# Expert stage of a two-block network: another transpose for short experts, and a third matrix half in high and low parts

## The chip, the cores and the metric

One Trainium2 chip, one of its cores. The metric is device time in microseconds of one execution of the whole program. Three runs of the kernel before took 1997.23, 2000.67 and 2002.16 us; their median is 2000.67 us.

## The reference, cut to what matters

256 tokens of width 1024 pass through two blocks. The change lies in the last large stage of the second block, a mixture of 8 experts, each of which has three matrices of 1024 x 3584, 1024 x 3584 and 3584 x 1024 in float32 (44 MB an expert, 352 MB in all):

```python
def moe_swiglu(h, w_router, w1, w3, w2):
    t = h.reshape(B * S, D)                                  # 256 x 1024
    logits = (t @ w_router).astype(jnp.float32)              # 8 experts
    top_vals, top_idx = lax.top_k(logits, TOP_K)             # TOP_K = 2
    top_w = jax.nn.softmax(top_vals, axis=-1)
    gates = jnp.sum(jax.nn.one_hot(top_idx, N_EXPERTS_2) * top_w[..., None], axis=1)
    out = jnp.zeros_like(t)
    for e in range(N_EXPERTS_2):
        out = out + gates[:, e:e + 1] * ((jax.nn.silu(t @ w1[e]) * (t @ w3[e])) @ w2[e])
    return out.reshape(B, S, D)
```

So 512 (token, expert) pairs are spread over 8 experts, some of which get more than 64 tokens and some fewer.

## The kernel before, in words

**Numbers in two parts.** TensorE takes float32 in a fast single pass only as fp32r, a float32 with a shortened mantissa. To keep precision the kernel splits an operand into `hi` (ScalarE copies it to fp32r, L99) and `lo` (VectorE subtracts `hi` from it, L100); `K.split` (L88) does both. A product is then hi·hi + hi·lo + lo·hi. A plain float32 product needs no split, but each of its matmuls goes through the array several times.

**Half-experts.** The stage, `moe` (L1508), handles each expert e in two halves s of 1792 hidden columns: 16 half-experts, n = 2e + s. For each there are three kinds of work, cut into jobs of two weight tiles of 128 x 1792 (896 KB each):
- *up*, 8 jobs: four for w1, then four for w3 (`up`, L1615, by `piece`, L1601). Each weight tile is loaded by a DMA on SP's queue (L85) into one of `RAW` = 9 places, split into one of 4 `whi` and one of 4 `wlo` places, and multiplied with the gathered token columns `xg`, which were split before. The four banks of results are copied out by ScalarE (`evict`, L1825): `gs` after w1, `us` after w3.
- *turn*, 4 groups of up to 4 column blocks (`turn`, L1634): `gs` and `us` are transposed on TensorE into two PSUM banks; then `turned` (L1816) makes silu of the one on ScalarE (L1822), multiplies it by the other on VectorE (L1823), and writes the block of `hd`, of which there is one place.
- *down*, 4 jobs (`down`, L1620): the weight tiles of w2 stay float32, are not split, and are multiplied with `hd` by plain float32 matmuls (L1629). Their place among the 9 is held until those matmuls are done.

**Short and long form.** The counts of the tokens are known only at run time. `arms` (L1594) makes a branch on TensorE alone: `many` (over 64 tokens) or `few`. For few tokens, the gathered columns lie so that token s of the first 64 is column 2s; `piece` then picks the 64 hi and the 64 lo columns as one stationary operand of 128, and two matmuls, with w hi and w lo, do what takes three in the long form. The result has 128 rows, 64 from hi and 64 from lo, whose sum is wanted. In `few`, `turn` (L1639) therefore doesn't transpose by the identity: it multiplies by `both` (L1520), in which column 2s has ones at rows s and 64 + s, and the other columns are zero, as a plain float32 matmul. So each transposed block comes out already summed. In `many` it is a plain transpose (L1641). `down` in `few` uses 64 stationary columns, and lets matmuls alternate between the two halves of the PSUM rows; the two halves are added when the result is sent back to the tokens (`transposed`, L1643, and `finish`, L1669).

**Order.** The list `jobs` (L1783) has, for each half-expert n: the 4 jobs of w1, the 4 of w3, and then the 4 down jobs of half-expert n - 1. `ahead` loads and splits one job ahead of the job being multiplied. The turn groups of n - 1 are put in front of the 4 w1 jobs of n; for even n they are branches of their own, so the scheduler may set the first group in the middle of the down jobs of n - 2. A scheduler sets the final order on each engine; ScalarE, VectorE and SP then work strictly in that order, waiting on semaphores. PSUM has 8 banks: 4 for an up product, 2 for a turn group and, for half of the time, 2 for the running down sums of an expert.

Of the kernel before, what the change touches and what calls it, by code (L numbers as in the profile page):

```python
# [8 lines left out]
F32 = mybir.dt.float32  # L9
# [10 lines left out]
P = 128  # L20
# [1105 lines left out]
ORD = (0, 1, 2, 3)  # L1126
RAW = 9


class Block2:  # L1130
# [378 lines left out]
    def moe(self, cap=P):  # L1509
# [8 lines left out]
        iota = iota_row(K, self.pool, P)  # L1518

        both = self.T([P, P])  # L1520
        nc.gpsimd.memset(both[:, 1::2], 0.0)
        nc.vector.tensor_tensor(both[:, 0::2], K.ident[:, :HALF], K.ident[:, HALF:], op=ADD)
        up_of = lambda n, e, s, k: a[n][0, e, k * P:(k + 1) * P, s * MS:(s + 1) * MS]
# [96 lines left out]
        def down(few, s, hd, acc, j, w):  # L1620


            c0 = c = j % 4 * MS
            while c < c0 + MS:
                c1 = min((c // 512 + 1) * 512, c0 + MS)
                r, h = divmod(c // 512, 2)
                o = slice((r + h) % 2 * HALF, (r + h) % 2 * HALF + HALF) if few else slice(0, P)
                n = 2 if few else 1
                mm(acc[h][o, c % 512:c % 512 + c1 - c], hd[:, j // 4 * R + r, ::n], w[0][:, c - c0:c1 - c0],  # L1629
                   start=s == 0 and j < 4 and r < n and c % 512 == 0,  # L1630
                   stop=s == NS - 1 and j > 3 and r >= R - n and c1 % 512 == 0)
                c = c1

        def turn(few, rows, pt, c0):  # L1634

            for c in range(c0, min(c0 + 4, 2 * R)):
                z = rows[:, c // R * (MS // 2) + c % R:(c // R + 1) * (MS // 2):R]
                if few:
                    mm(pt[:, (c - c0) * P:(c - c0 + 1) * P], z, both, start=True, stop=True)  # L1639
                else:  # L1640
                    nc.tensor.transpose(pt[:, (c - c0) * P:(c - c0 + 1) * P], z, K.ident)  # L1641

# [131 lines left out]
        def take(n, e, s, k, **how):  # L1774
            w = K.load(down_of(e, s, k) if n == "down" else up_of(n, e, s, k), 1, MS)
            if n == "down":
                return k, [w[:, 0]]
            b = lambda z: z.rearrange("p k (b q) -> p (k b) q", b=4)
# [4 lines left out]
        for i in range(E * NS + 1):  # L1783
# [3 lines left out]
            if i:  # L1787
                jobs += [("down", *divmod(i - 1, NS), (q, q + 1)) for q in range(0, 8, 2)]
        taken = {}
# [14 lines left out]
        for t in range(NT):  # L1804
            with K.behind(K.last):
                top2_weights(K, self.tmp, *tops[t][:2], iota, comb[:, t, :])
                nc.gpsimd.tensor_scalar(x[:, t, :], x[:, t, :], ALPHA, None, op0=MUL)
        most, mosti = self.T([P, 1]), self.T([P, 1], I32)
        nc.vector.tensor_reduce(most, cnt, axis=AX.X, op=MAX)
# [6 lines left out]
        def turned(i, c, pts):  # L1816

            n = min(4, 2 * R - c) * P
            if c == 0:
                hT[i] = self.W([P, 2 * R, P], "hd", F32, 1)  # L1820
            sg = self.W([P, 512], "sg", bufs=1)
            nc.scalar.activation(sg[:, :n], pts[0][:, :n], AF.Silu)  # L1822
            nc.vector.tensor_tensor(hT[i].rearrange("p c s -> p (c s)")[:, c * P:c * P + n], sg[:, :n], pts[1][:, :n], op=MUL)  # L1823

# [6 lines left out]
        for n, (name, e, s, ks) in enumerate(jobs):  # L1831
# [4 lines left out]
            if name == "down":  # L1836
                if s == 0 and q == 0:
                    accs[e] = [K.ps() for _ in range(2)]
                if i == E * NS - 1 and q == 0:
                    for c in range(0, 2 * R, 4):  # L1840
# [3 lines left out]
                arms(e, lambda few: [down(few, s, hT[i], accs[e], *t) for t in tiles])  # L1844
                if s == NS - 1 and q == 4:
                    hotT = transposed(e, gs[e][1])
                if s == NS - 1 and q == 6:
                    if e == E - 1:
# [109 lines left out]
```

## Time and profile before

| | |
|---|---|
| median of 3 runs | 2000.67 us |
| the profiled execution | 1999.19 us, of which the span of the profile is 1997.6 us |
| TensorE matmul (PE) busy in the span | 1843.4 us, 92% |
| VectorE (DVE) busy | 1133.8 us, 57% |
| ScalarE (ACT) busy | 929.9 us, 47% |
| DMA | 546.58 MB, mean 274 GB/s |
| TensorE's mean granted clock | 0.958 of full |

The expert stage runs from about 930 us to 1957 us of the span. Of its 8 experts, 0, 1 and 4 ran the long form and 2, 3, 5, 6, 7 the short one (lines L1613 and L1641 against L1610 and L1639). In this document, **stretch n** is the time from the eviction of `us` of half-expert n - 1 to that of half-expert n. It holds mostly the down jobs of n - 2, the turns of n - 1 and the up jobs of n:

| stretch | down | turn | up | us |
|---|---|---|---|---|
| 1 to 4 | many | many | many, many, many, few | 246.6 in all |
| 5 | many | few | few | 68.9 |
| 6 | few | few | few | 59.5 |
| 7 | few | few | few | 57.3 |
| 8 | few | few | many | 66.7 |
| 9 | few | many | many | 60.7 |
| 10 | many | many | few | 61.7 |
| 11 | many | few | few | 68.8 |
| 12 to 15 | few | few | few | 233.7 in all |
| the end | few (two) | few | none | 43.7 |

In odd stretches, VectorE and ScalarE also send the finished expert back to its tokens, and the next expert's tokens are gathered.

How to read the rows below. A row of a table of *windows* has: start:end of the window and its length in us; then for each engine its busy us in it and, in brackets, how many instructions ran (PE is matmuls, PEld weight loads); then the granted clock of TensorE (1.00 is full), the mean busy share of the DMA engines and what they moved in GB/s. A row of a *timeline* has: start and duration in us, engine, line, operation, output <- inputs, shapes, how many in a row, and in square brackets the idle time before it and what ended that. A row of the *chain of waits* has start, us, and what the end of the program hung on in that time. A row of *groups by line and shape* has the line, engine, operation, output <- inputs, shapes and the count; after the bar, busy us and the mean ns of one, and after the second bar the idle time before them and what ended it. A row of *waits* has who waited for whom, us in total, times, and the longest.

### The profile page before, as it was taken

To read this page: it belongs to the slowest core of one execution; us is meant where nothing else is said; L and a number is where in the kernel's file an instruction comes from. 1 tells how busy PE (TensorE), PEld (TensorE's weight loads), DVE (VectorE), ACT (ScalarE), POOL (GpSimd) and SP (SyncE) were. 2 spreads that over 40 slices of the span, in tenths; PEclk is the share of its full clock that TensorE was granted. 3 is DMA by queue.
4 is the path that set the end of the run, shared out by engine and by line. 5 is a ranking of instruction groups with operands and counts; after the bars stand their busy time and mean duration, and the time that the engine had idled before them with its cause. 6 is when DMAs were issued, how large, how long until landed. Compare 5 with 4: busy or idle time off the path is not lost. (4 is left out here: it accounts for less than half of the span.)

```text
span 1997.6 us, 27678 instructions
## 1 busy us (share of the span) xinstructions
PE 1843.4 (92%) x11023; PEld 1450.1 (73%) x11023; DVE 1133.8 (57%) x1395; ACT 929.9 (47%) x1222; POOL 169.8 (9%) x251
## 2 busy tenths in 40 slices
PE   7988698877999999987999999999999999999997
PEld 6878464323779998776877677877878678787875
DVE  4765542111986555887756436656557455675635
ACT  6444341101474443555746445545555445565533
POOL 2051210000400000324100000000000000000002
PEclk9989789889999999998999999999999999999999
DMA  7000579999655554415888989899989898999982
GB/s 221 29 1 1 193 292 407 421 421 397 243 179 175 190 190 148 169 43 219 323 299 318 327 273 376 319 362 395 360 326 400 306 361 308 387 376 359 405 318 106
DMA packets 131002, 546.58 MB, mean 274 GB/s; under 512 B 13568, under 2 KB 46475, under 8 KB 118540
## 3 DMA queue, kind: packets, MB, share of 16 engines
q1 hardware_dynamic: 126604, 539.21, 71.6%
q10 hardware_dynamic: 3952, 3.84, 0.6%
q8 instruction: 129, 2.11, 0.4%
q0 software_dynamic: 272, 1.05, 0.2%
q14 instruction: 45, 0.37, 0.1%
HBM read 543.01 MB, written 1.05 MB: 272 GB/s over the span
## 5 line engine op out<-in xcount | busy, mean ns | idle before, releaser
L100 DVE TENSOR_TENSOR wlo<-raw,whi 128x1792 fp32r<-128x1792 f32 (+2 forms) x412 | 681.0, 1694 | 291.5 <-ACT whi L99 290.2
L99 ACT ACTIVATE whi<-raw 128x1792 fp32r<-128x1792 f32 (+3 forms) x436 | 582.1, 1382 | 175.6 <-DMA raw<-in_exp_w_dram 59.2
L1610 PE MATMUL ps<-wlo,xg 128*128 128x256 f32 (+1 forms) x960 | 266.5, 308 | 17.0 <-DVE wlo L100 16.7
L1629 PE MATMUL ps<-raw,hd 128*64 128x512 f32 (+3 forms) x1024 | 275.4, 541 | 0.9 <-DVE hd L1823 0.9
L1610 PE MATMUL ps<-whi,xg 128*128 128x256 f32 (+1 forms) x960 | 266.7, 308 | 0.0
L1613 PE MATMUL ps<-whi,xg 128*128 128x512 f32 (+1 forms) x768 | 225.3, 373 | 0.0
L1629 PEld LDWEIGHTS ps<-raw,hd 128*64 128x64 f32 (+1 forms) x1024 | 129.5, 158 | 127.5 <-issue 111.8
L1610 PEld LDWEIGHTS ps<-wlo,xg 128*128 128x128 f32 x960 | 187.8, 196 | 33.5 <-DVE wlo L100 27.2
L1610 PEld LDWEIGHTS ps<-whi,xg 128*128 128x128 f32 x960 | 188.8, 197 | 9.6 <-issue 2.9
L114 PE MATMUL ps<-xTl,whi 128*128 128x256 f32 x576 | 161.4, 282 | 1.4 <-DVE xTl L100 1.4
L1613 PEld LDWEIGHTS ps<-whi,xg 128*128 128x128 f32 x768 | 141.6, 190 | 27.5 <-issue 1.5
L115 PE MATMUL ps<-xTh,wlo 128*128 128x256 f32 x544 | 153.4, 283 | 3.3 <-DVE wlo L100 3.2
L113 PE MATMUL ps<-xTh,whi 128*128 128x256 f32 x544 | 151.4, 281 | 0.4 <-ACT xTh L99 0.4
L1613 PE MATMUL ps<-wlo,xg 128*128 128x512 f32 (+1 forms) x384 | 141.7, 369 | 0.7 <-DVE wlo L100 0.7
L100 POOL TENSOR_TENSOR wlo<-raw,whi 128x448 fp32r<-128x448 f32 (+3 forms) x24 | 39.4, 1666 | 1105.7 <-ACT whi L99 1105.6
L1823 DVE TENSOR_TENSOR hd<-sg,ps 128x512 f32<-128x512 f32 x64 | 39.5, 617 | 127.2 <-PE ps L1629 88.7
L114 PEld LDWEIGHTS ps<-xTl,whi 128*128 128x128 f32 x576 | 108.7, 189 | 3.5 <-DVE xTl L100 2.7
L1822 ACT ACTIVATE sg<-ps 128x512 f32<-128x512 f32 x64 | 34.5, 539 | 162.0 <-PE ps L1639 91.6
L115 PEld LDWEIGHTS ps<-xTh,wlo 128*128 128x128 f32 x544 | 104.0, 191 | 5.7 <-DVE wlo L100 5.6
L113 PEld LDWEIGHTS ps<-xTh,whi 128*128 128x128 f32 x544 | 102.3, 189 | 1.7 <-ACT xTh L99 0.9
L1105 PE MATMUL ps<-dn,hT 128*32 128x512 f32 x256 | 70.3, 664 | 19.2 <-DMA dn<-in_w_down_dram 19.2
L1613 PEld LDWEIGHTS ps<-wlo,xg 128*128 128x128 f32 x384 | 73.0, 190 | 15.0 <-DVE wlo L100 1.2
(525 smaller groups left out, 2722.9 us busy)
## 6 DMA issues: line engine op xcount, KB each, us to landing
raw<-in_exp_w_dram SPq DMA_DIRECT2D x384, 896.0 KB
raw<-in_dense_w_dram SPq DMA_DIRECT2D x33, 1024.0 KB
gu<-in_w_up_dram SPq DMA_DIRECT2D x32, 1024.0 KB
dn<-in_w_down_dram SPq DMA_DIRECT2D x32, 1024.0 KB
gu<-in_w_gate_dram SPq DMA_DIRECT2D x29, 1024.0 KB
raw<-in_w_in_dram SPq DMA_DIRECT2D x19, 1024.0 KB
raw<-in_w_out_dram SPq DMA_DIRECT2D x8, 1024.0 KB
raw<-in_ple_gate_w_dram SPq DMA_DIRECT2D x8, 1024.0 KB
```

Source lines behind the costliest of these rows:

```text
L99: self.last = [nc.scalar.activation(hi[o], src[o], AF.Copy).ins, (engine or nc.vector).tensor_tensor(lo[o], src[o], hi[o], op=SUB).ins]
L100: (engine or nc.vector).tensor_tensor(lo[o], src[o], hi[o], op=SUB).ins]
L113: mm(out, a[0], b[0], start=first, stop=False)
L114: mm(out, a[0], b[1], start=False, stop=False)
L115: return mm(out, a[1], b[0], start=False, stop=last).ins
L1105: nc.tensor.matmul(ps[32 * e:32 * e + 32, :], hT[:, k, 32 * e:32 * e + 32], wd[e][:, k, hs], start=(k == 0), stop=(k == 1))
L1610: mm(to[:, o:o + m], few_rows, w[q][:, i.start + o:i.start + o + m], start=first and o == 0 and q == 0, stop=last and o + m == n and q == 1)
L1613: mm(to, rows[:, a_], w[b_][:, i], start=first and q == 0, stop=last and q == 2)
L1629: mm(acc[h][o, c % 512:c % 512 + c1 - c], hd[:, j // 4 * R + r, ::n], w[0][:, c - c0:c1 - c0], start=s == 0 and j < 4 and r < n and c % 51 ...
L1822: nc.scalar.activation(sg[:, :n], pts[0][:, :n], AF.Silu)
L1823: nc.vector.tensor_tensor(hT[i].rearrange("p c s -> p (c s)")[:, c * P:c * P + n], sg[:, :n], pts[1][:, :n], op=MUL)
```

## The change

It does four things, all in `moe`. (1) `turn` uses the plain transpose in both forms; in `few` its output columns are written with a step of two, so that the row 64i + s of the product lands in column 2s + i. `turned` then adds, in PSUM, the odd columns onto the even ones, for both banks of each group: ScalarE copies the odd columns to a tile `odd0` or `odd1`, scaled by `fewer` (1 for a short expert, 0 for a long one), and VectorE adds that to the even columns. (2) The weight tiles of w2 that belong to the first half of a half-expert's hidden columns (k < 4) are split as those of w1 and w3, and multiplied by `piece`; the matching 7 of the 14 blocks of `hd` are split too, into the new tile `hT`. The tiles with k >= 4 stay float32. (3) The down jobs of the second half-expert of each expert (s = 1) come in the order 4, 6, 0, 2, those of the first in the old order 0, 2, 4, 6. (4) `RAW` is 8 instead of 9.

```diff
@@ -1124,7 +1124,7 @@
 V4B = 2
 WHO = "avapavapavapavap"
 ORD = (0, 1, 2, 3)
-RAW = 9
+RAW = 8
 
 
 class Block2:
@@ -1516,10 +1516,6 @@
         MS, R = 1792, 7
         BANKS = ((0, 512), (512, 512), (1024, 512), (1536, 256))
         iota = iota_row(K, self.pool, P)
-
-        both = self.T([P, P])
-        nc.gpsimd.memset(both[:, 1::2], 0.0)
-        nc.vector.tensor_tensor(both[:, 0::2], K.ident[:, :HALF], K.ident[:, HALF:], op=ADD)
         up_of = lambda n, e, s, k: a[n][0, e, k * P:(k + 1) * P, s * MS:(s + 1) * MS]
 
         def down_of(e, s, j):
@@ -1620,25 +1616,26 @@
         def down(few, s, hd, acc, j, w):
 
 
-            c0 = c = j % 4 * MS
+            c0, c, cuts = j % 4 * MS, j % 4 * MS, 0
             while c < c0 + MS:
                 c1 = min((c // 512 + 1) * 512, c0 + MS)
                 r, h = divmod(c // 512, 2)
-                o = slice((r + h) % 2 * HALF, (r + h) % 2 * HALF + HALF) if few else slice(0, P)
-                n = 2 if few else 1
-                mm(acc[h][o, c % 512:c % 512 + c1 - c], hd[:, j // 4 * R + r, ::n], w[0][:, c - c0:c1 - c0],
-                   start=s == 0 and j < 4 and r < n and c % 512 == 0,
-                   stop=s == NS - 1 and j > 3 and r >= R - n and c1 % 512 == 0)
+                i, to = slice(c - c0, c1 - c0), acc[h][:, c % 512:c % 512 + c1 - c]
+                if j < 4:
+                    cut = c1 - c == 512 and cuts < 2
+                    cuts += cut
+                    piece(few, hd[0][:, r], w, i, to, s == 0 and r == 0, s == NS - 1 and r == R - 1, cut)
+                else:
+                    o = slice(h * HALF, h * HALF + HALF) if few else slice(0, P)
+                    mm(to[o], hd[1][:, R + r, ::2 if few else 1], w[0][:, i], start=False, stop=False)
                 c = c1
 
         def turn(few, rows, pt, c0):
 
             for c in range(c0, min(c0 + 4, 2 * R)):
                 z = rows[:, c // R * (MS // 2) + c % R:(c // R + 1) * (MS // 2):R]
-                if few:
-                    mm(pt[:, (c - c0) * P:(c - c0 + 1) * P], z, both, start=True, stop=True)
-                else:
-                    nc.tensor.transpose(pt[:, (c - c0) * P:(c - c0 + 1) * P], z, K.ident)
+                o = pt[:, (c - c0) * P:(c - c0 + 1) * P]
+                nc.tensor.transpose(o.rearrange("p (s i) -> p i s", i=2) if few else o, z, K.ident)
 
         def transposed(e, h):
 
@@ -1774,7 +1771,7 @@
         def take(n, e, s, k, **how):
             w = K.load(down_of(e, s, k) if n == "down" else up_of(n, e, s, k), 1, MS)
             if n == "down":
-                return k, [w[:, 0]]
+                return k, [z[:, 0] for z in (K.split(w) if k < 4 else (w,))]
             b = lambda z: z.rearrange("p k (b q) -> p (k b) q", b=4)
             hl = K.split(b(w), **how)
             return k, [z.rearrange("p b q -> p (b q)") for z in hl]
@@ -1785,7 +1782,8 @@
             if i < E * NS:
                 jobs += [(n, e, s, (q, q + 1)) for n in ("exp_w1_2", "exp_w3_2") for q in range(0, KC, 2)]
             if i:
-                jobs += [("down", *divmod(i - 1, NS), (q, q + 1)) for q in range(0, 8, 2)]
+
+                jobs += [("down", *divmod(i - 1, NS), (q, q + 1)) for q in ((0, 2, 4, 6), (4, 6, 0, 2))[(i - 1) % NS]]
         taken = {}
 
         def ahead(n):
@@ -1805,6 +1803,8 @@
             with K.behind(K.last):
                 top2_weights(K, self.tmp, *tops[t][:2], iota, comb[:, t, :])
                 nc.gpsimd.tensor_scalar(x[:, t, :], x[:, t, :], ALPHA, None, op0=MUL)
+        fewer = self.T([P, E])
+        nc.vector.tensor_scalar(fewer, cnt, HALF + 0.5, None, op0=ALU.is_lt)
         most, mosti = self.T([P, 1]), self.T([P, 1], I32)
         nc.vector.tensor_reduce(most, cnt, axis=AX.X, op=MAX)
         nc.vector.tensor_copy(mosti, most)
@@ -1816,11 +1816,20 @@
         def turned(i, c, pts):
 
             n = min(4, 2 * R - c) * P
+            for b, pt in enumerate(pts):
+                z = pt[:, :n].rearrange("p (c s i) -> p c s i", i=2, s=HALF)
+                odd = self.W([P, 4, HALF], f"odd{b}", F32, 1)[:, :n // P]
+                nc.scalar.activation(odd, z[:, :, :, 1], AF.Copy, scale=fewer[:, i // NS:i // NS + 1])
+                nc.vector.tensor_tensor(z[:, :, :, 0], z[:, :, :, 0], odd, op=ADD)
             if c == 0:
-                hT[i] = self.W([P, 2 * R, P], "hd", F32, 1)
+                hT[i] = (self.W([P, R, 2, P], "hT", F32R, 1), self.W([P, 2 * R, P], "hd", F32, 1))
+            hl, hd = hT[i]
             sg = self.W([P, 512], "sg", bufs=1)
             nc.scalar.activation(sg[:, :n], pts[0][:, :n], AF.Silu)
-            nc.vector.tensor_tensor(hT[i].rearrange("p c s -> p (c s)")[:, c * P:c * P + n], sg[:, :n], pts[1][:, :n], op=MUL)
+            nc.vector.tensor_tensor(hd.rearrange("p c s -> p (c s)")[:, c * P:c * P + n], sg[:, :n], pts[1][:, :n], op=MUL)
+            m = min(n // P, R - c)
+            if m > 0:
+                K.split(hd[:, c:c + m], hi=hl[:, c:c + m, 0], lo=hl[:, c:c + m, 1])
 
         def evict(banks, tag):
             z = self.W([P, MS], tag, F32, 1)
@@ -1836,15 +1845,15 @@
             if name == "down":
                 if s == 0 and q == 0:
                     accs[e] = [K.ps() for _ in range(2)]
-                if i == E * NS - 1 and q == 0:
+                if i == E * NS - 1 and q == 4:
                     for c in range(0, 2 * R, 4):
                         pts = [K.ps() for _ in range(2)]
                         arms(e, lambda few: [turn(few, rows, pt, c) for rows, pt in zip(ups[i], pts)])
                         turned(i, c, pts)
                 arms(e, lambda few: [down(few, s, hT[i], accs[e], *t) for t in tiles])
-                if s == NS - 1 and q == 4:
+                if s == NS - 1 and q == 0:
                     hotT = transposed(e, gs[e][1])
-                if s == NS - 1 and q == 6:
+                if s == NS - 1 and q == 2:
                     if e == E - 1:
                         finish_last(e, accs.pop(e), hotT)
                     else:
```

## Rows read from the trace of the kernel before

**Rows 1.** Windows: the expert stage, stretches 1 to 4, then 5 to 10.

```profile
990.00:1957.00 967.00, 944.71 (x4933) 743.48 (x4931) 552.03 (x408) 492.34 (x468) 0.00 (x0) 1.00 0.91 343
989.90:1236.50 246.60, 243.18 (x1147) 185.11 (x1146) 140.83 (x102) 126.86 (x121) 0.00 (x0) 0.99 0.88 319
1236.50:1305.40 68.90, 68.90 (x355) 55.65 (x354) 39.16 (x30) 34.18 (x35) 0.00 (x0) 1.00 0.92 333
1305.40:1364.90 59.50, 56.17 (x317) 45.31 (x316) 34.93 (x25) 31.53 (x29) 0.00 (x0) 1.00 0.93 359
1364.90:1422.20 57.30, 57.30 (x354) 49.27 (x353) 39.16 (x30) 34.12 (x35) 0.00 (x0) 1.00 1.00 398
1422.20:1488.90 66.70, 65.99 (x315) 51.63 (x314) 34.84 (x25) 31.95 (x28) 0.00 (x0) 1.00 0.88 335
1488.90:1549.60 60.70, 60.70 (x325) 47.32 (x325) 39.26 (x30) 34.15 (x34) 0.00 (x0) 1.00 0.96 382
1549.60:1611.30 61.70, 57.80 (x288) 42.42 (x288) 34.84 (x25) 31.53 (x29) 0.00 (x0) 1.00 0.88 325
```

**Rows 2.** Windows: stretches 12 to 15, and the end.

```profile
1680.10:1913.80 233.70, 224.63 (x1303) 186.02 (x1302) 146.48 (x104) 130.02 (x121) 0.00 (x0) 0.99 0.96 375
1913.80:1957.50 43.70, 41.74 (x194) 25.30 (x192) 3.39 (x7) 4.04 (x9) 0.00 (x0) 1.00 0.64 235
```

**Rows 3.** The chain of waits, stretch 13: a short turn, a short up job.

```profile
1763.01 3.70 PE ps L1639 x16
1766.70 3.33 PE ps L1610 x24
```

**Rows 4.** Timeline of PE, stretch 3: a long turn, up job, next turn.

```profile
1127.83 0.64 PE L1641 MATMUL ps<-t,gs 128*128 128x128 f32 x4
...
1128.71 0.48 PE L1613 MATMUL ps<-whi,xg 128*128 128x512 f32 x1
...
1133.71 0.65 PE L1641 MATMUL ps<-t,gs 128*128 128x128 f32 x4
```

**Rows 5.** Timeline of PE: four down jobs, long (stretch 3), short (stretch 13).

```profile
1103.78 24.21 PE L1629 MATMUL ps<-raw,hd 128*128 128x512 f32 x64
...
1740.66 12.31 PE L1629 MATMUL ps<-raw,hd 128*64 128x512 f32 x64
```

**Rows 6.** Groups by line and shape, 930 to 1960: splits, products, silu.

```profile
L100 DVE TENSOR_TENSOR wlo<-raw,whi 128x1792 fp32r<-128x1792 f32 x252 | 499.4, 2021 | 214.2 <-ACT whi L99 212.9 <-ACTq L1699 0.9
L99 ACT ACTIVATE whi<-raw 128x1792 fp32r<-128x1792 f32 x252 | 419.2, 1702 | 118.3 <-DMA raw<-in_exp_w_dram 59.2 <-PE ps L1613 34.6 <-PE ps L1610 23.3
...
L1823 DVE TENSOR_TENSOR hd<-sg,ps 128x512 f32<-128x512 f32 x48 | 32.8, 683 | 110.0 <-PE ps L1629 88.7 <-PE ps L1639 20.0 <-ACT sg L1822 1.4
L1822 ACT ACTIVATE sg<-ps 128x512 f32<-128x512 f32 x48 | 28.5, 593 | 134.7 <-PE ps L1639 71.5 <-PE ps L1641 42.2 <-DVE hd L1823 20.3
...
L1823 DVE TENSOR_TENSOR hd<-sg,ps 128x256 f32<-128x256 f32 x16 | 6.7, 418 | 17.1 <-PE ps L1639 15.2 <-ACT sg L1822 1.8
```

**Rows 7.** Groups by line and shape: a copy from PSUM scaled by a column.

```profile
L1050 ACT ACTIVATE xg<-ps,t 128x256 f32<-128x256 f32 x16 | 7.6, 473 | 16.1 <-PE ps L1046 16.1
```

**Rows 8.** Windows: a stretch of time in which the DMA engines never rest.

```profile
1375.00:1410.00 35.00, 35.00 (x206) 32.21 (x203) 27.85 (x22) 23.51 (x22) 0.00 (x0) 1.00 1.01 418
```

**Rows 9.** Waits: SP for places, ScalarE for weights, VectorE for the place of hd.

```profile
SPq L85 <- DVE wlo L100: 772.2, 242, 22.5
...
DVE hd L1823 <- PE ps L1629: 88.7, 8, 26.9
...
ACT whi L99 <- DMA raw<-in_exp_w_dram: 59.2, 29, 6.6
```

**Rows 10.** Timeline of DVE: hd waits in stretch 6, and at the end.

```profile
1323.66 0.69 DVE L1823 TENSOR_TENSOR hd<-sg,ps 128x512 f32<-128x512 f32 x1 [7.22 <-PE ps L1629]
...
1939.93 0.69 DVE L1823 TENSOR_TENSOR hd<-sg,ps 128x512 f32<-128x512 f32 x1 [26.90 <-PE ps L1629]
```

**Rows 11.** Windows: five us in stretch 13 with less than the full clock.

```profile
1755.00:1760.00 5.00, 4.29 (x21) 4.29 (x22) 4.22 (x3) 2.48 (x3) 0.00 (x0) 0.66 1.01 415
```

## The prediction

> **What bounds the kernel now.** I read the windows first, stage by stage, because shares of the whole span mix stages with different limits. In the expert stage TensorE's matmuls fill 944.7 of 967.0 us at full clock, while VectorE is at 552.0, ScalarE at 492.3, and the DMA engines show a share of 0.91 [rows 1]. Stretch by stretch there are two pictures. Where the long form runs or a short turn meets long down jobs (5, 8, 9), PE has no gap to speak of: 68.9 of 68.9, 66.0 of 66.7, 60.7 of 60.7. Where all is short (6, 7, 12 to 15), PE is just as full, 56.2 of 59.5 and 57.3 of 57.3, but the DMA share stands at 0.93 and 1.00 [rows 1, 2]. So PE is the bound throughout, and in the short stretches the transfers are right behind it. Then I read what PE does: a short turn group takes 3.70 us beside an up job of 3.33 [rows 3], a long one only 0.88, from 1127.83 to 1128.71 [rows 4]. Last I read what waits there are, because these grow when PE gets faster: VectorE stood 88.7 us before `hd`, whose one place the down jobs still read, and ScalarE 59.2 us for weights [rows 9].
>
> **PE, removed.** A short half-expert has 3.5 turn groups. At 3.70 us they cost 12.9, as plain transposes 3.5 x 0.88 = 3.1: 9.9 less, ten times [rows 3, 4]. A long down job costs 24.21 / 4 = 6.05 us; split, it is the same three products of two tiles as a long up job, 5.00 us from 1128.71 to 1133.71, so two jobs per half-expert save 2.1, six times [rows 4, 5]. A short down job costs 12.31 / 4 = 3.08 and becomes 3.33 like a short up job: 0.5 more per half-expert, ten times [rows 3, 5]. In all PE loses 99 + 12.6 - 5 = 107 us of work. If PE were the only bound, that would be the gain.
>
> **VectorE, added,** per half-expert. Four more `lo` of 2.02 us: 8.1. Eight additions of odd columns: six like the 256-column product of 0.418, and two of 128 columns, 0.28 each by the slope between 0.418 and 0.683: 3.1 in all. The `lo` of 512 and 384 columns of `hd`, 0.68 and 0.55: 1.2 [rows 6]. Sum 12.4: even short stretches go from 34.9 to 47.3, odd ones from 39.2 to 51.6 [rows 1].
>
> **ScalarE, added.** Four `hi` at 1.70 are 6.8 [rows 6]; six copies of odd columns at 0.473, scaled by a column as they are, and two at about 0.37 by the same slope, are 3.6 [rows 7]; two `hi` of `hd` at about 0.6 and 0.5 are 1.1. Sum 11.5, to 43 to 46 us a stretch, which hides behind VectorE.
>
> **The new chain in each group.** Transposes, copy, addition, silu, product, `hi`, `lo` go back and forth between two engines that work in order. VectorE waits for silu (0.59, less an addition of 0.42 beside it) and for `hi` (0.6). If the scheduler puts other splits there the loss is 0. If the queue goes group by group, the first `hi` of the next job starts only behind this group's last ScalarE step; a w1 job then lasts 8.0, 7.9, 6.8 and 6.4 us, 29.1 for four, against 23.0 of VectorE's own work (8 x 2.02, 3.1, products 2.5, `lo` 1.2): a loss of 6.1 a stretch [rows 6]. I take 2.5, the silu and `hi` waits alone, since today's order already lets splits run ahead.
>
> **DMA.** The bytes stay: 24 tiles of 917,504 B a stretch, and where the engines never rest they move 418 GB/s [rows 8], so 52.7 us is the least a stretch can last. Eight places instead of nine take one tile of lead, 0 to 2.2 us a stretch; but half of the down tiles now give their place back when split instead of when multiplied. I take 0. The loads of odd half-experts only change their order on SP's queue, and POOL loses one memset ahead of the stage: nothing. The order 4, 6, 0, 2 lets PE multiply unsplit tiles (6.2 us) while VectorE splits the others (8.1); without that cover it would cost about 2.
>
> **The sum.** Each stretch lasts as long as its highest floor and 3.3 us, which is what stretch 6 shows above its PE time today (59.5 - 56.2) [rows 1].
> Short, even: floors PE 56.2 - 9.9 + 0.5 = 46.8, VectorE 47.3 + 2.5 = 49.8, DMA 52.7; so 56.0. Odd: VectorE 51.6 + 2.5 = 54.1; so 57.4. Stretch 6 gains 3.5, stretch 7 nothing, 12 to 15 go from 233.7 to 226.8 [rows 1, 2]: -10.4.
> 5 and 11: PE 68.9 - 9.9 - 2.1 = 56.9; 60.2: -8.7 each, -17.4. 8: PE 66.0 - 9.4 = 56.6; 59.9: -6.8. 9: +0.5. 10: -2.1. 1 to 4, PE-bound with three long down groups: -6.3.
> The end: `hd` waited 26.90 us there for the down jobs before it [rows 10], beside 12.9 us of short turns. Now 12.8 of down jobs, 2.6 of transposes, about 4 for three products and silus in turn before the first down job can read its blocks, and 12.8: some 9.5 less on 43.7 [rows 2]; I take 9.
> Total -51.5. The profiled execution took 1999.2 (span 1997.6), 1.5 under the median, so 1947.7 by its own time and **1949** by the median. Of 107 us taken from PE half is given back, to DMA and VectorE, in the short stretches.
>
> **A rule against it.** All transposes in the trace write neighbouring columns; the new ones, for few tokens, write every second. Their price lies between 0.88 us a group, the plain ones, and 3.70, the product they replace [rows 3, 4]; nearest is the plain one, the same instruction. Twice 0.88 would be covered in short stretches and show in 5, 8 and 11 alone: 9 us, 1958. The Trainium skill, in "PSUM — Partial Sum Buffer", section Specifications, says PSUM is organised in 8-byte lines and that a non-contiguous pattern slows matmuls significantly; a step of two float32 would be such a pattern, and by that rule the sum would be nearer 1958 than 1949. No run shown here has such a write.
>
> **Rivals.**
> *All cover holds (0.12).* The scheduler interleaves perfectly: no chain wait, no 3.3. Short stretches fall to 52.7, 5 and 11 to 56.9, 8 to 56.6, 10 to 55.7, 1 to 4 by 9.7 and the end by 10: -94, 1907. For it: stretch 7 already runs without a gap on PE [rows 1]. Against: VectorE would be 98% busy in odd stretches.
> *VectorE's queue becomes the bound (0.17).* Its place is `hd` in even stretches: VectorE is next in line for the product, the place is still read by down jobs, and the `lo` of the next weights stand behind it, as at 1323.66, 7.22 us [rows 10]. Seven such waits take 88.7 - 26.9 = 61.8, or 8.8 each [rows 9, 10]. Today that is hidden because VectorE has 24 us to spare; with 47.3 of work it isn't. With the serial chain, even short stretches last 47.3 + 6.1 + 8.8 + 3.3 = 65.5 and odd ones 61.0. Against today that is +6.0, +3.7 and +19.3 (6, 7, 12 to 15), +3.8 each for 4 and 10, -7.9 each for 5 and 11, -1.2 for 8, +0.5 for 9, -4.2 for 1 to 3, -5 at the end: +11. While VectorE stands, no place comes free, and with one place fewer a tile of 2.2 us is late after each: +15. So +26, 2027. It decides from the point at which waits inside VectorE's queue pass 59.5 - 3.3 - 47.3 = 8.9 us in an even stretch.
> *The two cancel (0.08).* Half of that: about 2000.
> *The strided transpose is no cheaper than the product (0.07).* Then only the long down jobs gain, 12.6 less some 3 for the rest: about 1991.
>
> TensorE's clock stays out of the sum. It was full but for 0.66 in five microseconds after a gap [rows 11]; if more gaps in the short stretches halve it for moments, that lies under the DMA floor.
>
> **How the numbers follow.** The forecast has 0.56, and its own range is 1925 to 1985, by chain waits of 0 to 6.1 and 0 to 5 above the floor. The range 1912 to 2012 leaves out the lower half of the first rival and two thirds of the second, some 0.17. About 0.3%, 6 us, is what a measurement tells from no change. Faster: forecast, first and last rival, 0.75; same 0.08; slower 0.17.
>
> **What would show it.** Right: short turn groups near 0.9 us; PE busy in the stage some 100 us lower, with gaps in short stretches; their DMA share at 1.00 and VectorE at 47 to 52; stretches 5, 8 and 11 shortened most, 7 hardly, the end by about 9. Wrong: turn groups of 2 us or more; VectorE's wait for `hd` above 89 us in total; PE waiting for `wlo` for several us in w1 jobs; long down jobs not at 5.0.

## The result, and the profile after

The changed kernel takes 1965.39 us in the median of 4 runs (1962.56 to 1969.16), the kernel before in the same job 1998.95: a ratio of 0.9834, with a 95% interval of 0.9807 to 0.9861. The whole interval lies below 1, so the gain of 1.7% is clear of the noise; the time is inside the range and 16 us above the forecast: 33.6 us gained of 51.5. The profiled execution took 1963.39 us (span 1961.8).

The windows first, with the columns of [rows 1, 2]: the stage, stretches 1 to 4 together, 5 to 11 one by one, 12 to 15 together, the end.

```profile
988.36:1920.50 932.14, 870.01 (x4909) 711.73 (x4908) 733.78 (x632) 655.72 (x695) 0.00 (x0) 0.97 0.93 358
988.36:1237.64 249.28, 239.43 (x1195) 192.80 (x1195) 179.04 (x154) 161.78 (x173) 0.00 (x0) 0.99 0.87 317
1237.64:1304.62 66.98, 63.27 (x356) 52.44 (x355) 53.25 (x46) 48.80 (x51) 0.00 (x0) 0.95 0.94 353
1304.62:1355.74 51.12, 46.10 (x290) 38.48 (x289) 43.41 (x38) 36.84 (x40) 0.00 (x0) 0.97 0.99 397
1355.74:1414.27 58.53, 53.84 (x357) 46.43 (x355) 53.13 (x46) 48.94 (x52) 0.00 (x0) 0.97 1.01 410
1414.27:1472.65 58.38, 55.99 (x289) 44.81 (x288) 43.49 (x38) 37.18 (x41) 0.00 (x0) 0.97 0.98 378
1472.65:1536.27 63.62, 63.21 (x350) 51.83 (x349) 53.27 (x46) 49.16 (x52) 0.00 (x0) 1.00 0.91 355
1536.27:1596.25 59.98, 55.04 (x296) 44.46 (x295) 43.58 (x38) 36.80 (x41) 0.00 (x0) 0.97 0.90 333
1596.25:1664.14 67.89, 62.55 (x356) 51.60 (x355) 53.30 (x46) 48.89 (x51) 0.00 (x0) 0.97 0.93 349
1664.14:1885.64 221.50, 198.32 (x1245) 167.08 (x1244) 190.24 (x160) 170.94 (x178) 0.00 (x0) 0.96 0.99 393
1885.64:1920.52 34.88, 32.25 (x193) 21.80 (x191) 21.04 (x25) 16.40 (x26) 0.00 (x0) 1.00 0.85 328
```

PE no longer fills its stage: 870.0 of 932.1 us, against 944.7 of 967.0 [rows 1]. The short stretches became short and are at the transfers' limit (a DMA share of 0.98 to 1.01 in 6, 7, 8 and 12 to 15), as forecast. The surprise is the second row: stretches 1 to 4, of long half-experts, where PE has the most to do and was to lose 6.3 us of it, got *longer*, 249.3 after 246.6, with 10 us in which PE stands. The granted clock is below full in nearly every stretch, 0.97 over the stage; before, it was 1.00 over the stage and 0.99 in the lowest rows [rows 1, 2].

The scheduler moved some down jobs across the evictions that bound the stretches, so neighbours are compared in pairs. (Stretch 6 alone lasts 51.1 us, less than the 52.7 called the least, because it moves 397 GB/s x 51.12 us = 20.3 MB and not 22.0.) "The end" runs here from the last eviction of `us` to the last matmul of the stage, 46.6 us before. Change against the kernel before, in us, from the times of the evictions in each profiled execution; the experiments stand beside it and come below.

| stretches | forecast | changed kernel | turn only (e2) | split only (e3) | no additions for long (e5) | banks out early (e6) |
|---|---|---|---|---|---|---|
| 1 to 4 | -6.3 | +2.6 | +10.2 | -5.4 | -5.2 | -5.0 |
| 5, 6 | -12.2 | -10.2 | -9.3 | -2.7 | -10.8 | -12.2 |
| 7, 8 | -6.8 | -7.1 | -5.9 | +0.8 | -7.7 | -8.8 |
| 9, 10 | -1.6 | +1.1 | +5.9 | -2.5 | -0.7 | -0.4 |
| 11 to 15 | -15.6 | -13.1 | -19.6 | -0.7 | -13.0 | -16.2 |
| the end | -9 | -9.3 | -6.3 | -1.2 | -9.4 | -5.1 |
| sum | -51.5 | -36.0 | -25.0 | -11.7 | -46.8 | -47.7 |

Next the timeline, for the prices, in three excerpts: a long turn group and the split down job behind it, a long turn group that stands, and a short turn group.

```profile
1040.24 0.64 PE L1638 MATMUL ps<-t,gs 128*128 128x128 f32 x4
...
1041.12 0.48 PE L1609 MATMUL ps<-whi,hT 128*128 128x512 f32 x1
...
1079.20 0.66 PE L1638 MATMUL ps<-t,us 128*128 128x128 f32 x4
1079.46 0.97 ACT L1822 ACTIVATE odd<-ps,t 128x256 f32<-128x256 f32 x2 [3.48 <-PE ps L1638]
1079.97 0.93 DVE L1823 TENSOR_TENSOR ps<-ps,odd 128x256 f32<-128x256 f32 x2 [1.80 <-ACT odd L1822]
1080.33 1.69 ACT L99 ACTIVATE whi<-raw 128x1792 fp32r<-128x1792 f32 x1
1081.91 0.59 ACT L1828 ACTIVATE sg<-ps 128x512 f32<-128x512 f32 x1
1082.05 2.03 DVE L100 TENSOR_TENSOR wlo<-raw,whi 128x1792 fp32r<-128x1792 f32 x1 [1.15 <-ACT whi L99]
...
1082.56 0.51 PE L1638 MATMUL ps<-t,gs 128*128 128x128 f32 x2 [2.69 <-ACT sg L1828]
...
1083.99 0.68 DVE L1829 TENSOR_TENSOR hd<-sg,ps 128x512 f32<-128x512 f32 x1
...
1084.82 0.68 PE L1638 MATMUL ps<-t,us 128*128 128x128 f32 x2 [1.75 <-DVE hd L1829]
...
1307.28 0.64 PE L1638 MATMUL ps<-t,gs 128*128 128x128 f32 x4
...
1308.16 0.38 PE L1606 MATMUL ps<-whi,hT 128*128 128x256 f32 x1
```

The short group at 1307.28 writes every second column, the long one at 1040.24 neighbouring columns; each takes 0.88 us to the next start, where the product took 3.70 [rows 3]. So the strided write costs nothing in these transposes. The Trainium skill, in "PSUM — Partial Sum Buffer", section Specifications, says that any non-contiguous pattern slows matmuls significantly; this trace doesn't agree, by these two rows.

The middle excerpt is the new loss. PE has turned a long group by 1079.86. Its banks come free in turn: the bank of `gs` after two copies, two additions, a `whi` of 1.69 us that ScalarE had queued in between, and the silu; the bank of `us` only after a `wlo` of 2.03 us on VectorE and the product. PE stands 2.69 us for the one and 1.75 for the other. A long group needs no addition at all: its factor is 0.

The groups by line and shape of VectorE and ScalarE in the stage, answering to [rows 6, 7]:

```profile
L100 DVE TENSOR_TENSOR wlo<-raw,whi 128x1792 fp32r<-128x1792 f32 x302 | 602.0, 2019 | 125.3 <-ACT whi L99 120.5 <-ACTq L1696 4.2 <-DVEq L1696 0.4
L1823 DVE TENSOR_TENSOR ps<-ps,odd 128x256 f32<-128x256 f32 x96 | 38.7, 425 | 4.9 <-ACT odd L1822 4.6
L1829 DVE TENSOR_TENSOR hd<-sg,ps 128x512 f32<-128x512 f32 x48 | 32.8, 683 | 40.8 <-PE ps L1630 38.7 <-ACT sg L1828 0.7
...
L1823 DVE TENSOR_TENSOR ps<-ps,odd 128x128 f32<-128x128 f32 x32 | 8.4, 291 | 2.6 <-ACT odd L1822 2.1
```

```profile
L99 ACT ACTIVATE whi<-raw 128x1792 fp32r<-128x1792 f32 x302 | 505.8, 1706 | 65.9 <-PE ps L1609 37.3 <-PE ps L1606 17.1 <-DMA raw<-in_exp_w_dram 8.8
L1822 ACT ACTIVATE odd<-ps,t 128x256 f32<-128x256 f32 x96 | 43.0, 468 | 20.0 <-PE ps L1638 19.6 <-DVE ps L1823 0.2
```

The unit prices were right: 425 and 291 ns an addition (0.418 and 0.28 forecast), 468 a copy (473). VectorE's wait for the place of `hd` didn't grow, it fell from 88.7 us [rows 9] to 38.7, and ScalarE's wait for weights from 59.2 to 8.8.

Last PE's waits in the stage, answering to [rows 9]:

```profile
PE ps L1606 <- ACT sg L1828: 13.4, 7, 2.4
PE ps L1606 <- DVE wlo L100: 9.0, 14, 0.7
PE ps L1638 <- DVE t L1661: 8.6, 7, 1.6
PE ps L1638 <- DVE hd L1829: 8.1, 7, 1.7
PE ps L1656 <- ACT sg L1828: 7.0, 5, 1.4
PE ps L1638 <- ACT sg L1828: 4.8, 3, 2.7
...
PE ps L1609 <- ACT sg L1828: 2.4, 1, 2.4
```

Every line but that of `wlo` is a wait for a PSUM bank that another engine still reads: silu 27.6 us, product 8.1, the addition back into `x` 8.6, 44.3 in all. Before, PE had none of these in the stage; it waited for low parts, for operands and once at a branch (2.7 us). The first row of its waits before:

```profile
PE ps L1610 <- DVE wlo L100: 16.7, 19, 1.7
```

### The profile page after: what moved, and what is told of

Its sections match the earlier page's. It is cut to its first block, busy times and chain, and to the rows that moved or that the text cites. A ratio compares the mean times of both kernels' runs of the same rounds, so it can differ in the third digit from the quotient of the medians.

```text
span 1961.8 us, 28227 instructions
## 1 busy us (share of the span) xinstructions
PE 1768.9 (90%) x10999; PEld 1421.1 (72%) x10999; DVE 1315.1 (67%) x1619; ACT 1092.3 (56%) x1446; POOL 169.4 (9%) x250
## 5 line engine op out<-in xcount | busy, mean ns | idle before, releaser
L100 DVE TENSOR_TENSOR wlo<-raw,whi 128x1792 fp32r<-128x1792 f32 (+2 forms) x476 | 811.6, 1736 | 212.5 <-ACT whi L99 207.5
L99 ACT ACTIVATE whi<-raw 128x1792 fp32r<-128x1792 f32 (+3 forms) x500 | 692.5, 1425 | 136.5 <-PE ps L1609 49.3
L1606 PE MATMUL ps<-whi,xg 128*128 128x256 f32 (+1 forms) x960 | 279.1, 319 | 14.0 <-ACT sg L1828 13.4
L1606 PE MATMUL ps<-wlo,xg 128*128 128x256 f32 (+1 forms) x960 | 276.5, 317 | 6.9 <-DVE wlo L100 6.5
L1606 PEld LDWEIGHTS ps<-whi,xg 128*128 128x128 f32 x960 | 196.9, 205 | 27.8 <-ACT sg L1828 15.3
L1606 PEld LDWEIGHTS ps<-wlo,xg 128*128 128x128 f32 x960 | 196.4, 205 | 21.9 <-DVE wlo L100 14.7
L1609 PEld LDWEIGHTS ps<-whi,xg 128*128 128x128 f32 x768 | 143.0, 192 | 30.7 <-ACT sg L1828 2.6
L1630 PE MATMUL ps<-raw,hd 128*64 128x512 f32 (+3 forms) x512 | 137.6, 542 | 2.1 <-DVE hd L1829 2.1
L1630 PEld LDWEIGHTS ps<-raw,hd 128*64 128x64 f32 (+1 forms) x512 | 62.8, 158 | 64.6 <-issue 54.5
L1609 PEld LDWEIGHTS ps<-wlo,xg 128*128 128x128 f32 x384 | 73.7, 192 | 13.9 <-issue 0.5
L1822 ACT ACTIVATE odd<-ps,t 128x256 f32<-128x256 f32 (+1 forms) x128 | 53.7, 442 | 36.2 <-PE ps L1638 35.8
L1606 PE MATMUL ps<-wlo,hT 128*128 128x256 f32 (+1 forms) x240 | 67.8, 313 | 5.4 <-issue 2.9
```

The lines of the kernel that those rows point to most:

```text
L99: self.last = [nc.scalar.activation(hi[o], src[o], AF.Copy).ins, (engine or nc.vector).tensor_tensor(lo[o], src[o], hi[o], op=SUB).ins]
L100: (engine or nc.vector).tensor_tensor(lo[o], src[o], hi[o], op=SUB).ins]
L1606: mm(to[:, o:o + m], few_rows, w[q][:, i.start + o:i.start + o + m], start=first and o == 0 and q == 0, stop=last and o + m == n and q == 1)
L1609: mm(to, rows[:, a_], w[b_][:, i], start=first and q == 0, stop=last and q == 2)
L1630: mm(to[o], hd[1][:, R + r, ::2 if few else 1], w[0][:, i], start=False, stop=False)
L1822: nc.scalar.activation(odd, z[:, :, :, 1], AF.Copy, scale=fewer[:, i // NS:i // NS + 1])
```

## The experiments

The theory after these readings: the two parts took nearly the forecast from the turns and long down jobs, but the chain of a turn group (transposes, copy, addition, silu, product, with splits of weights queued between its steps) holds its two banks for some 3 to 5 us, and with four banks of the up jobs and two of the down jobs in use PE has nowhere to write. The rival: the floors of the transfers and of VectorE, and PE would gain nothing from freer banks.

**e1, the additions out.**

```diff
-            for b, pt in enumerate(pts):
-                z = pt[:, :n].rearrange("p (c s i) -> p c s i", i=2, s=HALF)
-                odd = self.W([P, 4, HALF], f"odd{b}", F32, 1)[:, :n // P]
-                nc.scalar.activation(odd, z[:, :, :, 1], AF.Copy, scale=fewer[...])
-                nc.vector.tensor_tensor(z[:, :, :, 0], z[:, :, :, 0], odd, op=ADD)
```

> Left out: the ScalarE copies of the odd columns and the VectorE additions, so the halves of few rows are not summed; everything else is done. Theory (the chain of a turn group, transposes, copy, addition, silu, product, holds its two PSUM banks, and PE stands behind it): PE's waits for silu, product and additions, 44 us in the changed kernel, fall to about 20, and the time falls by 10 to 20 us, to 1945 to 1955. Rival (the floors of the transfers and of VectorE set the stretches): only VectorE's 3.1 us per half-expert go, PE's waits turn into waits for low parts, and the time stays at 1958 to 1966.

Measured 1953.47 us, ratio 0.9774 (0.9753 to 0.9794): some 12 us below the changed kernel, by the ratios. PE's waits in its stage:

```profile
PE ps L1606 <- DVE wlo L100: 28.1, 37, 1.7
PE ps L1606 <- DVE t L1661: 8.8, 5, 1.8
PE ps L1609 <- DVE wlo L100: 4.0, 3, 1.5
...
PE ps L1638 <- DVE hd L1824: 1.7, 3, 0.7
```

The waits for silu and product all but go, 44.3 us of bank waits become 10.7 (8.8 for the addition back into `x`, 1.7 for the product, 0.2 for silu); those for low parts rise from 9.0 to 32.1. Both halves of the argument are there: the banks decided, and the other floor is right behind. Stretches 1 to 4 fall to 241.4 us. It fits the theory, but the run also takes work off two engines.

**e2 and e3, the two parts alone.** e2 is the kernel before with the new `turn` and the additions, and 8 places; e3 is the changed kernel with the old `turn` and without the additions. Of e3's edit, the turn:

```diff
-                nc.tensor.transpose(o.rearrange("p (s i) -> p i s", i=2) if few else o, z, K.ident)
+                if few:
+                    mm(pt[:, (c - c0) * P:(c - c0 + 1) * P], z, both, start=True, stop=True)
+                else:
+                    nc.tensor.transpose(pt[:, (c - c0) * P:(c - c0 + 1) * P], z, K.ident)
```

> The plain transposes with added halves alone; the third matrix unsplit in the old order, 8 places. Theory (the turn is most of the gain, the split a small part): PE busy in the stage falls by 75 to 85 us, the long stretches 1 to 4 gain nothing, and the time is 1960 to 1975. Rival (without the split the one place of the product's result stays with eight down jobs, and the turn groups stand behind it, PE with them): PE waits for the product of 40 us and more on top, and the time is 1980 to 2000.

> The split half of the third matrix, its order and the 8 places alone; the turn of few rows is the product with the matrix of two identities as before. Theory: PE loses 12.6 us in long down jobs and gets 5 to 9 us more in short ones, VectorE has 9.3 us more per half-expert under a full PE: 1985 to 2000. Rival (the split, by freeing the product's place, is the gain): 1965 to 1980.

Measured: e2 1973.69 us, ratio 0.9877 (0.9858 to 0.9897); e3 1988.55, ratio 0.9957 (0.9940 to 0.9974). Both theories' times came. The product of the ratios, 0.9834, is the whole change, so in total the parts add up. Stretch by stretch they don't: in 5, 6 and in 11 to 15 e2 and e3 together gain 32.3 us and the whole change 23.3, and in each of the other rows the whole change is about 2 us better than the two together. So in the short stretches the parts hinder each other. In the table, e3 gains 5.4 us in stretches 1 to 4, nearly the 6.3 forecast from the long down jobs; e2 *loses* 10.2 there, where its turn brings nothing and the additions run all the same. PE's busy time fell by 70.5 us in e2 (947.3 to 876.8), a little less than the 75 to 85 expected. The rival of e2, turn groups standing behind the one place of the product, is out: VectorE's wait for it was 49.7 us, down from 88.7, and PE's for a bank that the product still reads 5.9.

**e4, the eviction of `gs` ahead of the last group's chain.**

```diff
-            if before:
-                turned(i - 1, 2 * q, pts)
             if q == 6:
                 z = evict(banks, "gs" if first else "us")
                 ups.setdefault(i, []).append(z)
+            if before:
+                turned(i - 1, 2 * q, pts)
```

> The changed kernel with the eviction of the first matrix's banks placed ahead of the last turn group's copies and silu on ScalarE. Theory (PE stands 2.4 us seven times before the third matrix's first up job, because its banks come free only behind that silu): the 13.4 us of that wait go to under 5, and the time falls by 4 to 12 us, to 1953 to 1961. Rival (another floor is right behind): the wait moves to low parts or to the turn group, and the time stays within 3 us of 1965.

Measured 1962.40 us, ratio 0.9823 (0.9807 to 0.9840), not to be told from the changed kernel. But the edit hardly reached its place. The seven waits of the expectation were in fact five of 2.4 us, one of 1.29 and one of 0.19; the five are all left, and at one of them, 1343.28, ScalarE still runs copy, `whi`, copy, silu and only then the four evictions: moving the statement did not move the work there. The run settles nothing.

**e5, no additions for the long experts.** The counts are known here ahead of time, so this is a measurement, not a kernel for other data:

```diff
-            for b, pt in enumerate(pts):
+            for b, pt in enumerate(pts if i // NS not in (0, 1, 4) else ()):
```

> The copies and additions of odd columns are left out for the experts 0, 1 and 4 alone (long form, whose additions have the factor zero, so that nothing of the result changes). Theory (in the long stretches the additions bring nothing and hold the two banks, so PE stands there): stretches 1 to 4 go from 249 us to 241 to 243, and the time falls by 7 to 12 us, to 1953 to 1958. Rival (only the short stretches lose by the chain): stretches 1 to 4 stay at 247 to 250 and the time within 4 us of 1965.

Measured 1954.87 us, ratio 0.9783 (0.9763 to 0.9804); stretches 1 to 4 take 241.4 us, 9 and 10 lose 1.8 more. So about 10 us of the 16 to 18 that are missing are lost on additions of nothing, in stretches in which the prediction had charged them at zero.

**e6, the banks out early.** The additions stay, for all experts, but ScalarE copies each bank whole to SBUF first:

```diff
+            full = []
...
-                odd = self.W([P, 4, HALF], f"odd{b}", F32, 1)[:, :n // P]
-                nc.scalar.activation(odd, z[:, :, :, 1], AF.Copy, scale=fewer[...])
-                nc.vector.tensor_tensor(z[:, :, :, 0], z[:, :, :, 0], odd, op=ADD)
+                full.append(self.W([P, 512], f"odd{b}", F32, 1)[:, :n])
+                nc.scalar.activation(full[b], pt[:, :n], AF.Copy)
+                z = full[b].rearrange("p (c s i) -> p c s i", i=2, s=HALF)
+                nc.vector.scalar_tensor_tensor(z[:, :, :, 0], z[:, :, :, 1], fewer[...], z[:, :, :, 0], op0=MUL, op1=ADD)
...
-            nc.scalar.activation(sg[:, :n], pts[0][:, :n], AF.Silu)
+            nc.scalar.activation(sg[:, :n], full[0], AF.Silu)
-            nc.vector.tensor_tensor(hd..., sg[:, :n], pts[1][:, :n], op=MUL)
+            nc.vector.tensor_tensor(hd..., sg[:, :n], full[1], op=MUL)
```

> Each group's two banks are copied whole to SBUF by ScalarE, and addition, silu and product work there, so that a bank is free after one copy instead of after copy, addition, silu and product; the additions stay. Theory (banks held by the chain are what PE stands behind): PE's waits for silu, product and additions, 44 us, fall below 25, and the time falls by 5 to 12 us, to 1953 to 1960. Rival (not the banks but the two engines' own time for the additions): the waits move to low parts of the weights and the time stays at 1961 to 1968.

Measured 1954.22 us, ratio 0.9776 (0.9760 to 0.9792), faster than the kernel before and, with no overlap of the intervals, than the changed kernel. This is the decisive run: it does *more* on both engines (VectorE 741.3 us in the stage against 736.1, ScalarE 671.0 against 657.7) and takes 11 us less, so it isn't the engines' time but the hold on the banks. PE's waits:

```profile
PE ps L1606 <- DVE wlo L100: 17.6, 37, 1.3
PE ps L1638 <- ACT odd L1822: 13.6, 18, 1.3
PE ps L1638 <- DVE t L1661: 10.3, 7, 1.9
PE ps L1630 <- DVE hd L1830: 4.3, 2, 3.4
```

None for silu is left; the copies have 13.6 us in 18 short waits in its place. With 10.3 for the addition back into `x` and 4.2 for an eviction, 28.1 us of bank waits are left of 44.3, and the waits for low parts grew from 9.0 to 17.6. In the table its column is the forecast's, within 2.0 us in each row but the last.

**e7, seven places for loads** (`RAW = 7`).

> Seven places for loads in place of eight. Theory (the places don't decide, PE stands behind banks): 0 to 4 us slower, 1965 to 1969. Rival (one tile of lead, 2.2 us, is lost in each of the ten short stretches): 10 to 25 us slower, 1975 to 1990.

Measured 1977.26 us, ratio 0.9897 (0.9881 to 0.9914), some 12 us slower: the size of the rival, but not its place. The profiled span grew by 13.0: only 3.3 in the expert stage (937.8 against 934.5), 6.6 behind it, and 3.1 ahead of it, where profiled executions of the same code differ by as much (the first eviction at 988.4 to 994.8 in the runs with eight places and this stage's new form). Behind the stage the gate's weights are loaded and split; with seven places, POOL gets to their low parts at 1940.68, with eight at 1922.24. The timelines, first of e7 (ScalarE, then POOL), then of the changed kernel (POOL):

```profile
1939.93 4.25 ACT L99 ACTIVATE whi<-raw 128x512 fp32r<-128x512 f32 x8
1940.68 10.68 POOL L100 TENSOR_TENSOR wlo<-raw,whi 128x512 fp32r<-128x512 f32 x8 [984.22 <-ACT whi L99]
```

```profile
1922.24 1.29 POOL L100 TENSOR_TENSOR wlo<-raw,whi 128x512 fp32r<-128x512 f32 x1 [968.91 <-PE ps L1656]
```

The loads themselves weren't issued later: the last went out at 1925.91, 3.9 us before the stage's last matmul, with eight places 4.2 us before it. ScalarE makes the eight `hi` behind work of the normalisation in e7, and the first of them ahead of it, at 1921.47, in the changed kernel. So the 6.6 us come with another order on ScalarE; how one place fewer led to that order isn't shown.

**e8, split and unsplit down jobs in turn.**

```diff
-... for q in ((0, 2, 4, 6), (4, 6, 0, 2))[(i - 1) % NS]]
+... for q in ((0, 4, 2, 6), (4, 0, 6, 2))[(i - 1) % NS]]
```

> Down jobs alternate between split and unsplit pairs: 0, 4, 2, 6 and 4, 0, 6, 2 in place of 0, 2, 4, 6 and 4, 6, 0, 2. Theory (the order of the down jobs matters little, the waits sit at the turn groups): within 4 us of 1965. Rival (four splits in a row are late for PE): 4 to 10 us faster.

Measured 1980.91 us, ratio 0.9905 (0.9888 to 0.9922): some 14 us slower by the ratios, 15.7 in the stage, and both expectations missed. PE's timeline of e8 has a float32 job alone, and one at the end with waits before it and in it:

```profile
1305.97 3.65 PE L1630 MATMUL ps<-raw,hd 128*64 128x512 f32 x16
...
1920.19 1.83 PE L1630 MATMUL ps<-raw,hd 128*64 128x512 f32 x4 [2.56 <-DVE hd L1829]
1923.19 4.77 PE L1630 MATMUL ps<-raw,hd 128*64 128x512 f32 x12 [1.17 <-DVE hd L1829]
```

A float32 job between two others takes 3.58 us to the next start, two in a row 6.22 (1311.90 to 1318.12 in the changed kernel): 0.94 us more per pair of jobs, 9.4 for ten short half-experts. The one at the end took 7.70 (1920.19 to 1927.89), 1.17 of it the wait, at a granted clock of 0.57 from 1920.1 to 1928.0. PE's waits for low parts rose as well, from 9.0 to 18.1 us, so how the 15 us are shared wasn't settled. Still, the neighbourhood of the unsplit jobs is worth something that no step had counted.

**e9, banks out early and the eviction first.** The edits of e6 and e4 together.

> The run with the banks copied out early, and with the eviction of the first matrix's banks placed ahead of the last group's copies. Theory (with the banks out early, 4.2 us of waits for that eviction are left, most of it under other floors): 1951 to 1955, at most 3 us below the run with the banks out early. Rival (the eviction decides now that the silu doesn't): 1945 to 1950.

Measured 1957.60 us, ratio 0.9785 (0.9761 to 0.9809): no gain on e6. The waits for the eviction are 4.1 us, as in e6 (4.2).

**e10, banks out early, and nothing at all for the long experts** (the copies and additions of e6 under `if i // NS not in (0, 1, 4)`).

> The banks copied out early, and for the experts 0, 1 and 4 no copies and no additions at all, silu and product from the banks as in the kernel before. Theory (what the additions cost in long stretches is the hold of the banks, which the early copies already end): stretches 1 to 4 stay at 240 to 243 and the time within 3 us of 1954. Rival (the two engines' own time for copies and additions costs there too): stretches 1 to 4 at 236 to 239, 1945 to 1950.

Measured 1956.73 us, ratio 0.9794 (0.9775 to 0.9812); stretches 1 to 4 take 241.5 us, e6 has 241.6. Once the banks are free early, the additions cost nothing in the long stretches. The rival is out.

**e11, the turn alone with nine places** (e2 with `RAW = 9`).

> The plain transposes with added halves alone, unsplit third matrix in the old order, with the nine places of the kernel before in place of eight. Theory (a place costs little inside the stage, as seven did against eight, and some microseconds behind it): 0 to 6 us faster than with eight, 1968 to 1974. Rival (each place is one tile of lead, worth the 12 us that the step from eight to seven cost): 1960 to 1964.

Measured 1979.62 us, ratio 0.9898 (0.9877 to 0.9919); with eight it was 0.9877 (0.9858 to 0.9897). That is above both expectations. The ninth place brought nothing; the intervals overlap, so it isn't shown that it costs anything either. For the turn alone, then, the step from nine to eight at nought was right, though in the changed kernel the one from eight to seven isn't free.

## Why the prediction was right, and where it fell short

**PE, removed.** The stage's matmuls, added up from the timeline from each start to the next start or, where earlier, its own end: turn groups 147.3 to 58.5 us, -88.8 (-99 forecast); long down jobs 142.3 to 129.5, -12.8 (-12.6); short down jobs 128.5 to 137.1, +8.6 (+5); all up jobs 488.9 to 503.6, +14.7 (0); the way back 15.4 to 18.5. In all -75, not -107. The prices at full clock held for the turn (0.88) and the long down job (4.99, from 1041.12 to 1046.11). A split short down job is 73.7 / 20 = 3.69 us and not the 3.33 of an up job, nearly all of that at full clock: two in a row took 6.77 (1363.04 to 1369.81), one alone 3.74 (1308.16 to 1311.90). A turn group beside a wait took more than 0.88, 1.17 at 1500.30. The 14.7 of the up jobs are matmuls at the lower clock. That PE's term was 32 us too large cost the sum less, since most short stretches were at the transfers' limit all the same.

**The clock** was left out, as something under the DMA floor, and as full but for one dip in a short stretch [rows 11]. The trace of before has a second one, in stretch 4, where PE is the bound, behind a gap of 1.67 us at 1218.90. Both windows show the lower of the two levels, the first of before, the second of the changed kernel behind a gap of 2.38 us at 1339.28:

```profile
1220.00:1223.00 3.00, 3.00 (x14) 2.81 (x13) 2.72 (x2) 3.00 (x5) 0.00 (x0) 0.50 1.02 373
```

```profile
1341.00:1344.00 3.00, 3.00 (x14) 2.81 (x13) 2.32 (x4) 3.00 (x3) 0.00 (x0) 0.50 1.02 418
```

The short up jobs' 256-column products took 290 to 291 ns before. The groups of the changed kernel's stage, and then those of e3, in which PE keeps the product and stands 22 us in the stage, as before:

```profile
L1606 PE MATMUL ps<-whi,xg 128*128 128x256 f32 x800 | 219.8, 301 | 14.0 <-ACT sg L1828 13.4
L1606 PE MATMUL ps<-wlo,xg 128*128 128x256 f32 x800 | 218.4, 299 | 6.9 <-DVE wlo L100 6.5
```

```profile
L1609 PE MATMUL ps<-wlo,xg 128*128 128x256 f32 x800 | 210.3, 291 | 13.2 <-DVE wlo L100 13.0
L1609 PE MATMUL ps<-whi,xg 128*128 128x256 f32 x800 | 210.0, 291 | 0.0
```

The granted clock of the stage is 0.97 to 0.98 in every run with the new turn and 1.00 in e3 and before. In the stretches 1 to 4 this is on the path: PE is busy 239.4 us, against 236.6 in e5 at clock 1.00. How much of the 14.7 us is on the path in the short stretches wasn't separated.

**The step that failed** is the one that priced the new chain. By it the chain costs VectorE 2.5 us in a short stretch, and the added 12.4 and 11.5 us of VectorE and ScalarE are otherwise hidden; stretches 1 to 4, "PE-bound with three long down groups: -6.3". So the additions were charged to the engine that runs them and only where that engine was near its limit. What the runs showed instead is that they are charged to PE, through the banks, and most of all where PE is the bound: +8 us in stretches 1 to 4 (249.3 against 241.4 in e5: 5.0 of it PE standing, 2.9 PE busy at the lower clock) and about 2 in 9 and 10. The 8 us aren't a fixed price: with all additions kept, stretches 1 to 4 took 244.9 us both in e7 and in e8, 3.5 above e5, so more than half of the 8 came with the changed kernel's own order of work (stretches 2 and 3 lasted 76.1 and 65.9 us in it, 65.7 and 71.9 in e7). The number of banks (four for the up jobs, two for the down jobs, two for a turn group) stood in the code and in no floor of the sum. With the hold shortened, e6 gives 1954.2 us, 5 above the forecast, and the forecast's own picture stretch by stretch.

A rule that would have pointed there: the Trainium skill, "Perfetto Trace Analysis", section Matmuls, asks that independent groups rotate through different banks, so that emptying one overlaps the next one's matmuls. The trace agrees: 44.3 us of waits for banks that another engine still read.

**The steps that held.** VectorE's and ScalarE's durations; the DMA floor in the short stretches (5 and 6 at -10.2 of -12.2, 7 and 8 at -7.1 of -6.8, 11 to 15 at -13.1 of -15.6); the end, -9.3 of -9; the places at nought, as far as e2 and e11 show. The order 4, 6, 0, 2 as a cover, priced at about 2 us, was not tested: e8 has a third order, and not the old one.

**The rivals.** *All cover holds*: no, PE stands 62 us. *VectorE's queue becomes the bound*: its sign, a wait for `hd` above 89 us, didn't come, the wait more than halved; but its picture, chain steps standing behind `wlo` in a queue that works in order, is what the excerpt at 1082.05 shows, only that PE pays there. *The strided transpose is no cheaper*, and the side case that it costs twice: out by 0.88 us in both forms.

## What to carry to other kernels

Work put between a matmul's result and the release of its PSUM bank was priced here not by the engine that does it but by how long the bank is held, and it cost most where PE is the bound; count banks as one counts places for loads, and copy a bank out first if the work behind it is long. Work that is the same for all cases of a branch (here additions with a factor of 0) should be priced in the case that gains nothing from it. A change can cost its price in the stage behind the one that was looked at (6.6 of e7's 13.0 us).

## What was not expected of the hardware

A float32 job of two tiles takes 3.58 us between jobs of the other type, and two in a row take 6.22 (e8 and the changed kernel; 64 stationary columns). With 128 stationary columns there is no such price: one job alone took 5.61 us from 1046.11 to the next start, two in a row 11.62 from 1188.10, so the change of number type alone doesn't explain it. The cause is open. Transposes that write every second float32 column of PSUM are as fast as those that write neighbours, 0.88 us for eight. With PE's gaps in the stage grown from 22 to 62 us in total, spread over all its stretches, the granted clock fell from 1.00 to 0.97, and products of unchanged shape got 3% longer (291 to 300 ns at 256 columns).
